# Weight blocks of twice the size in the merge of a hybrid encoder layer

## The chip, the cores and the metric

The kernel runs on one core of a Trainium2 chip. The metric is the device time of one execution in microseconds (us); the time before is the median of three runs. A further execution was recorded by the hardware profiler, and all rows come from it. The core's engines are TensorE (PE; its weight loads are shown as PEld), VectorE (DVE), ScalarE (ACT), GpSimd (POOL) and SyncE (SP, which here only issues transfers).

## The reference

One layer of a residual block on x of 2048 tokens by 1024 channels, float32:

```
h      = rms_norm(x, pre_mix_g)
proj   = h @ w_in                       # q, k, v | RWKV-7 inputs | two gates
y_a    = chunk_band_attention(q, k, v, rel_bias)
y_b    = rwkv7_time_mix(...)            # recurrent, a scan over time
merged = sigmoid(gA) * (y_a @ proj_a) + sigmoid(gB) * (y_b @ proj_b)
x      = x + rms_norm(merged @ w_out, post_mix_g)
hf     = rms_norm(x, pre_ffn_g)
x      = x + rms_norm(square(relu(hf @ w_up)) @ w_down, post_ffn_g)
```

proj_a and proj_b are 512 x 1024, and w_out is 1024 x 1024. The change concerns the lines `merged` and `merged @ w_out`.

## The kernel before

The tokens are worked in four groups of 512 (G). For each group come the recurrent part, the attention part and the merge; the feed-forward part follows once for each half of the tokens. Every product is made in three matmuls: an operand is kept as a rounded high part and a low part that holds the rest, and high x high, high x low and low x high are summed in PSUM (`mm3`, L74).

Weights come through `wsplit` (L58). It takes a raw buffer, loads the block on SP's queue (L63), and calls `split` (L69): ACT casts the block to the high part (whi, L70), DVE subtracts to get the low part (wlo, L71). Raw, high and low each have two buffers, shared by all weight blocks of this part of the program. A buffer is as large as its largest user, a block of `w_in` of 8 x 128 = 1,024 floats in each of 128 partitions.

The merge has two stages. In the first, `branch` (L1030) makes one block of 128 output channels of one branch: it loads the gate values (th, L1034, from gd), loads and splits a block of proj_b or proj_a of 4 x 128 = 512 floats a partition (L1035 and L1036), multiplies (12 matmuls of 512 columns into ps_p), and DVE applies the gate (L1039). `phase_attention` calls it eight times for the recurrent branch and stores the results (md, L1015) while the attention of the last heads still runs. `phase_merge` (L1042) calls it eight times for the attention branch, adds the stored result (mb, L1054 and L1056) and splits the sum into mh and ml (L1057). There are three buffers for th and three for mb.

In the second stage the output projection runs in two halves n of 512 columns, each over eight blocks k of w_out of 512 floats a partition (L1062), with 12 matmuls a block, three for each of four token tiles, into four PSUM banks (ps_o, L1066). At the end of a half ACT and DVE take the banks out (L1076, L1077).

Two other pieces of work are put between these blocks. `beside` is one set of operand sums for the feed-forward part (`combine`, L1110): its first step loads four tiles of 256 KB (cmb, L1145), its next three steps do one DVE subtraction each (L1117), and its fifth does the last one and stores four results on POOL's queue (L1141). `between` is `next_norm` (L295), the norm of the next group: its first step loads two tiles of x and the gains, 512 KB each (L302, L305), and each of the next four steps makes one tile (ACT L319, POOL, DVE L321, eight transposes on PE at L126, ACT L130 and DVE L131) and loads another tile of x while there is one. The last group has no next norm.

A scheduler orders the instructions of each engine by a simulated time, so that an instruction which is ready early may overtake others of its engine. Some are pinned: `keep_in_program_order` puts an instruction behind everything that was traced before it on its engine. The operand-sum loads, their DVE subtractions, the norm's loads and its first transposes are pinned so; weight, gate and mb loads are not. Each engine is given its instructions in the order that comes out of this.

Of the kernel before, what the change touches and what calls it, by code (L numbers as in the profile page):

```python
# [18 lines left out]
P = 128  # L19
D = 1024  # L20
KB = D // P
FF = 4096
HW = 512
NP = 4
# [18 lines left out]
def advance(steps, n=None):  # L43

    while n is None or n > 0:
        if next(steps, steps) is steps:
            return
        n = n and n - 1


class Block:
# [978 lines left out]
    def branch(self, y, br, i):  # L1030

        nc, mp = self.nc, self.bp
        t = mp.tile([P, G], F32, tag="th", bufs=3, name="th")
        nc.sync.dma_start(t, self.gd[br * KB + i])  # L1034
        w = self.a[("proj_a", "proj_b")[br]][:, i * P : (i + 1) * P]  # L1035
        wh, wl = self.wsplit(w.rearrange("(k p) n -> p k n", p=P), "w", NP, P)  # L1036
        ps = self.pd.tile([P, G], F32, tag="d", name="ps_p")
        self.mm3(ps, [(wh[:, k], wl[:, k], y[0][:, k], y[1][:, k]) for k in range(NP)])
        nc.vector.scalar_tensor_tensor(t, t, 1.0, ps, op0=ALU.add, op1=ALU.mult)  # L1039
        return t  # L1040

    def phase_merge(self, g, o, op, between, beside):  # L1042

        tc, nc, a = self.tc, self.nc, self.a
        with ExitStack() as ctx:
            e = ctx.enter_context
            cp = e(tc.tile_pool(name="mgc", bufs=1, reuse_waits="tile"))
            po = e(tc.tile_pool(name="mgpo", bufs=4, space=PSUM, reuse_waits="tile"))
            mh = cp.tile([P, KB, G], F32R, name="mh")
            ml = cp.tile([P, KB, G], F32R, name="ml")  # L1050
            gp = self.gain(op, a["post_mix_g"], "g_post")
            for i in range(KB):
                mb = self.bp.tile([P, G], F32, tag="mb", bufs=3, name="mb")
                nc.sync.dma_start(mb, self.md[i])  # L1054
                t = self.branch(self.ya, 0, i)
                nc.vector.tensor_tensor(t, t, mb, ALU.add)  # L1056
                self.split(mh[:, i], ml[:, i], t)  # L1057
            self.yctx.close()
            for n in range(2):
                ps = [po.tile([P, 512], F32, tag="o", name="ps_o") for _ in range(GT)]  # L1060
                for k in range(KB):
                    wh, wl = self.wsplit(a["w_out"][k * P : (k + 1) * P, None, n * 512 : (n + 1) * 512], "w", 1, 512)  # L1062
                    for t in range(GT):
                        ts = slice(t * P, (t + 1) * P)
                        for j, (l, r) in enumerate(((mh, wh), (mh, wl), (ml, wh))):
                            nc.tensor.matmul(  # L1066
                                ps[t], l[:, k, ts], r[:, 0], start=k == 0 and j == 0, stop=k == KB - 1 and j == 2
                            )
                    if n == 0 and k in (0, 3, 4, 5, 6):
                        advance(beside, 1)  # L1070
                    if n == 0 and k == 2 or n == 1 and k % 2 == 0:
                        advance(between, 1)
                ns = slice(n * 512, (n + 1) * 512)
                for t in range(GT):
                    sq = op.tile([P, 512], F32, tag="sqo", bufs=2, name="sqo")
                    nc.scalar.activation(sq, ps[t], AF.Square, accum_out=self.ssq[:, g, t, n : n + 1])  # L1076
                    nc.vector.tensor_tensor(o[t][:, ns], ps[t], gp[:, ns], ALU.mult)  # L1077
            advance(between)
# [426 lines left out]
```

## Time and profile before

| | us |
|---|---|
| median of three runs | 3324.03 (3318.0 to 3327.82) |
| the profiled execution's own time | 3325.37 |
| its span, first to last instruction | 3323.7 |
| PE busy | 3198.8 |
| DVE busy | 2248.2 |
| ACT busy | 1581.6 |
| POOL busy | 592.7 |
| output projection of the first group | 466.6 to 520.5 of the span |

In a row of groups, the source line, engine and operation come first, then what is written and read, the shape and the count; after the bar come busy time and mean duration in ns, and after the second bar the time that the engine idled just before these instructions, with what ended that idle time. In a timeline, a row has start, length, engine, line and tiles; "SPq" is an issue of a transfer by SP, not the transfer itself. Matmuls are pipelined and the profile models their ends, so PE's busy time is more than its work.

### The profile page before, as it was taken

The numbers are of one execution on the slowest core, as the hardware profiler recorded it, in microseconds if no ns is written. First come the engines' busy times: TensorE is split into PE (matmuls) and PEld (weight loads), VectorE is DVE, ScalarE is ACT, GpSimd is POOL, SyncE is SP. The second block draws the span as 40 slices with busy tenths as digits, with TensorE's granted clock in tenths as the row PEclk, the third lists the DMA queues.
The fourth block names the chain that finished last, engine by engine and source line by source line (L and its number), as shares of the span: only waits on it lengthen the run. The fifth ranks groups of instructions, "written<-read, shape, count | busy, mean of one in ns | idle before, by whom it ended". The sixth has DMA issues, their size and how long they took to land. (4 is left out here: it accounts for less than half of the span.)

```text
span 3323.7 us, 50325 instructions
## 1 busy us (share of the span) xinstructions
PE 3198.8 (96%) x18913; PEld 2597.9 (78%) x18913; DVE 2248.2 (68%) x3719; ACT 1581.6 (48%) x2575; POOL 592.7 (18%) x1093
## 2 busy tenths in 40 slices
PE   7999999999999999999999999999999999999998
PEld 5777778777877777877777787878788878788887
DVE  5775666786766876775876675777656757775565
ACT  3434634434644434654444663545543444454333
POOL 2222002222102222101222100121211112220000
PEclk9999999999999999999999999999999999999999
DMA  5335374247465336655325647664787875547565
GB/s 151 89 118 186 114 232 126 80 137 241 156 215 154 91 104 229 198 170 186 96 77 187 208 121 246 231 199 143 240 285 232 300 250 193 168 161 235 191 214 179
DMA packets 449692, 592.56 MB, mean 178 GB/s; under 512 B 26324, under 2 KB 313248, under 8 KB 449448
## 3 DMA queue, kind: packets, MB, share of 16 engines
q1 hardware_dynamic: 392488, 413.14, 40.1%
q0 software_dynamic: 47744, 159.42, 13.2%
q10 hardware_dynamic: 9216, 16.78, 1.4%
q8 instruction: 149, 2.44, 0.3%
q14 instruction: 95, 0.78, 0.1%
HBM read 425.37 MB, written 167.01 MB: 178 GB/s over the span
## 5 line engine op out<-in xcount | busy, mean ns | idle before, releaser
L1341 PE MATMUL ps_dn<-fop 128*128 128x512 f32 x2688 | 613.1, 390 | 2.3 <-DVE fop L71 1.5
L1341 PEld LDWEIGHTS ps_dn<-fop 128*128 128x128 f32 x2688 | 505.3, 188 | 108.2 <-DVE fop L71 2.2
L80 PE MATMUL psd<-hh,whi 128*128 128x512 f32 x1344 | 540.1, 402 | 10.8 <-ACT whi L70 7.6
L80 PE MATMUL psd<-hh,wlo 128*128 128x512 f32 x1344 | 538.1, 400 | 2.7 <-DVE wlo L71 2.6
L80 PE MATMUL psd<-hl,whi 128*128 128x512 f32 x1344 | 539.2, 401 | 0.0
L70 ACT CAST whi<-wraw 128x1024 fp32r<-128x1024 f32 (+1 forms) x296 | 255.5, 864 | 521.6 <-PE psd L80 337.2
L71 DVE TENSOR_TENSOR wlo<-wraw,whi 128x1024 fp32r<-128x1024 f32 (+1 forms) x296 | 292.8, 990 | 223.7 <-ACT whi L70 190.3
L80 PEld LDWEIGHTS psd<-hh,whi 128*128 128x128 f32 x1344 | 255.2, 190 | 61.7 <-ACT whi L70 8.4
L80 PEld LDWEIGHTS psd<-hh,wlo 128*128 128x128 f32 x1344 | 255.0, 190 | 55.1 <-DVE wlo L71 5.2
L80 PEld LDWEIGHTS psd<-hl,whi 128*128 128x128 f32 x1344 | 255.5, 190 | 48.9
L71 DVE TENSOR_TENSOR fop<-xraw,fop 128x1024 fp32r<-128x1024 f32 x112 | 137.1, 1224 | 175.0 <-ACT fop L70 174.3
L70 ACT CAST fop<-xraw 128x1024 fp32r<-128x1024 f32 x112 | 117.7, 1051 | 254.5 <-PE ps_dn L1341 187.5
L1223 POOL DMA_DIRECT2D xd<-X x192 | 103.7, 541 | 392.1 <-ACT X L1220 337.3
L71 DVE TENSOR_TENSOR fop<-wdraw,fop 128x1024 fp32r<-128x1024 f32 x112 | 136.7, 1221 | 23.5 <-ACT fop L70 22.7
L70 ACT CAST fop<-wdraw 128x1024 fp32r<-128x1024 f32 x112 | 117.7, 1051 | 39.8 <-DMA wdraw<-in_w_down_dram 26.1
L903 DVE CUSTOM_DVE_ANT_0 sc<-bias,ps_s 128x640 f32<-128x640 f32 (+4 forms) x128 | 94.0, 734 | 57.0 <-PE ps_pt L914 40.3
L919 DVE TENSOR_TENSOR PTl<-ps_pt,PTh 128x640 fp32r<-128x640 f32 (+4 forms) x128 | 94.4, 738 | 27.7 <-ACT PTh L918 27.2
L70 ACT CAST s12h<-s 128x1024 fp32r<-128x1024 f32 x32 | 33.7, 1052 | 163.7 <-PE ps_u L80 163.7
L908 ACT ACTIVATE sc<-sc,mn 128x640 f32<-128x640 f32 (+4 forms) x128 | 97.6, 762 | 26.1 <-DVE mn L903 25.7
L1066 PE MATMUL ps_o<-whi,mh 128*128 128x512 f32 x256 | 98.8, 400 | 10.2 <-ACT whi L70 8.5
L1066 PE MATMUL ps_o<-wlo,mh 128*128 128x512 f32 x256 | 101.8, 398 | 4.9 <-DVE wlo L71 4.8
L80 PE MATMUL ps_p<-yh,whi 128*128 128x512 f32 x256 | 101.3, 401 | 5.4 <-ACT whi L70 3.6
(368 smaller groups left out, 6823.5 us busy)
## 6 DMA issues: line engine op xcount, KB each, us to landing
wraw<-in_w_in_dram SPq DMA_DIRECT2D x168, 512.0 KB
xraw<-xd SPq DMA_DIRECT2D x112, 512.0 KB
xd<-X POOLq DMA_DIRECT2D x192, 256.0 KB, 5.3
wraw<-in_w_up_dram SPq DMA_DIRECT2D x80, 512.0 KB
wdraw<-wd SPq DMA_DIRECT2D x64, 512.0 KB
wdraw<-in_w_down_dram SPq DMA_DIRECT2D x48, 512.0 KB
gd<-gate ACTq DMA_DIRECT2D x64, 256.0 KB
wd<-cmb POOLq DMA_DIRECT2D x64, 256.0 KB, 3.5
```

The costliest lines, as they stand in the source:

```text
L70: high = self.nc.scalar.copy(hi, src)
L71: self.nc.vector.tensor_tensor(lo, src, hi.bitcast(F32), ALU.subtract)
L80: mm.append(nc.tensor.matmul(ps, l, r, start=n == 0, stop=n == last).ins)
L903: nc.vector.tensor_tensor_reduce(sc[:, 0:n], bias[:, s0:640], pss[:, c0 : c0 + n], 1.0, 3.0e38, ALU.add, ALU.min, mn,)
L908: nc.scalar.activation(sc[:, 0:n], sc[:, 0:n], AF.Exp, scale=-1.0, bias=mn, accum_out=sm[:, col : col + 1])
L919: nc.vector.tensor_tensor(lv, pst[:, 0:nk], hv.bitcast(F32), ALU.subtract)
L1066: nc.tensor.matmul(ps[t], l[:, k, ts], r[:, 0], start=k == 0 and j == 0, stop=k == KB - 1 and j == 2)
L1223: nc.gpsimd.dma_start(self.xd[q][i // 2][:, i % 2], src)
L1341: nc.tensor.matmul(ps, o[:, l, k, sl], o[:, r, k], start=start and n == 0, stop=stop and n == end)
```

## The change

Branch weights are loaded and split for two blocks i at a time, 4 x 256 floats a partition, and each of the two calls of `branch` uses its half. Blocks of the output projection are loaded and split for two k at a time, 2 x 512 floats. A block now fills its buffers. The numbers of matmuls and of floats loaded stay as they were. In the first half of the output projection the steps of the operand sums move from behind k = 0, 3, 4, 5, 6 to behind k = 2, 4, 5, 6, 7, and the first step of the next norm (its loads) moves from behind k = 2 to behind k = 4.

```diff
-        w = self.a[("proj_a", "proj_b")[br]][:, i * P : (i + 1) * P]
-        wh, wl = self.wsplit(w.rearrange("(k p) n -> p k n", p=P), "w", NP, P)
+        if i % 2 == 0:
+            w = self.a[("proj_a", "proj_b")[br]][:, i * P : (i + 2) * P]
+            self.bw = self.wsplit(w.rearrange("(k p) n -> p k n", p=P), "w", NP, 2 * P)
+        wh, wl = (x[:, :, i % 2 * P : (i % 2 + 1) * P] for x in self.bw)
...
                 for k in range(KB):
-                    wh, wl = self.wsplit(a["w_out"][k * P : (k + 1) * P, None, n * 512 : (n + 1) * 512], "w", 1, 512)
+                    if k % 2 == 0:
+                        w = a["w_out"][k * P : (k + 2) * P, n * 512 : (n + 1) * 512]
+                        wh, wl = self.wsplit(w.rearrange("(j p) n -> p j n", p=P), "w", 2, 512)
...
-                                ps[t], l[:, k, ts], r[:, 0], start=k == 0 and j == 0, stop=k == KB - 1 and j == 2
+                                ps[t], l[:, k, ts], r[:, k % 2], start=k == 0 and j == 0, stop=k == KB - 1 and j == 2
...
-                    if n == 0 and k in (0, 3, 4, 5, 6):
+                    if n == 0 and k in (2, 4, 5, 6, 7):
                         advance(beside, 1)
-                    if n == 0 and k == 2 or n == 1 and k % 2 == 0:
+                    if n == 0 and k == 4 or n == 1 and k % 2 == 0:
                         advance(between, 1)
```

## The prediction

> **What bounds the kernel now.** I read the page first, then the groups by line and form, the windows of the stages that the change touches, and the timelines of SP, ACT, DVE and PE inside one of them.
>
> ```profile
> span 3323.7 us, 50325 instructions
> PE 3198.8 (96%) x18913; PEld 2597.9 (78%) x18913; DVE 2248.2 (68%) x3719; ACT 1581.6 (48%) x2575; POOL 592.7 (18%) x1093
> L1066 PE MATMUL ps_o<-whi,mh 128*128 128x512 f32 x256 | 98.8, 400 | 10.2 <-ACT whi L70 8.5
> L80 PE MATMUL ps_p<-yh,whi 128*128 128x512 f32 x256 | 101.3, 401 | 5.4 <-ACT whi L70 3.6
> ```
>
> PE is busy in 96% of the span, so the number of matmuls sets the time, and an edit that removes no matmul can only win what PE idles. The change touches the branch products (ps_p) and the output projection (ps_o). There PE's idle time (the last column) ends with a cast (whi) or a subtraction (wlo) of a weight block. The answers on the two tiles give all of it for PE, in us and in number of stalls, and beside it stands how matmuls follow one another without a stall:
>
> ```profile
>   ACT whi L70: 8.5, 9
>   DVE wlo L71: 4.8, 7
> ...
>   ACT whi L70: 3.6, 5
> ...
>   DVE wlo L71: 0.3, 2
> ...
> 484.51 0.39 PE L1066 MATMUL ps_o<-whi,ml 128*128 128x512 f32 x1
> 484.74 0.39 PE L1066 MATMUL ps_o<-whi,mh 128*128 128x512 f32 x1
> 484.96 0.39 PE L1066 MATMUL ps_o<-wlo,mh 128*128 128x512 f32 x1
> 485.19 0.39 PE L1066 MATMUL ps_o<-whi,ml 128*128 128x512 f32 x1
> ```
>
> The first two rows are ps_o, the next two ps_p: 8.5 + 4.8 + 3.6 + 0.3 = 17.2 us. The other four rows show matmuls starting every (485.19 - 484.51) / 3 = 0.227 us while each is shown 0.39 long, so every stall really costs about 0.16 more than its idle time. The two stages look like this, four groups each (the branch stage first, then the output projection):
>
> ```profile
> 441.40:466.60 25.20, 23.38 (x96) 17.48 (x96) 18.74 (x29) 8.81 (x16) 0.54 (x1) 1.00 0.90 270
> 961.00:986.90 25.90, 25.04 (x105) 19.11 (x105) 19.03 (x31) 9.11 (x15) 1.08 (x2) 1.00 0.92 279
> 1475.00:1500.60 25.60, 25.23 (x107) 19.32 (x105) 19.43 (x31) 9.08 (x16) 1.08 (x2) 1.00 0.88 279
> 1997.00:2022.30 25.30, 24.03 (x104) 18.85 (x102) 18.38 (x30) 8.88 (x15) 0.85 (x2) 1.00 0.86 281
> 466.60:520.50 53.90, 50.26 (x226) 40.58 (x226) 29.65 (x42) 23.80 (x48) 5.62 (x14) 0.97 0.55 177
> 986.90:1037.80 50.90, 48.00 (x225) 39.12 (x225) 28.86 (x41) 23.34 (x47) 5.60 (x14) 1.00 0.56 180
> 1500.60:1553.50 52.90, 48.64 (x226) 39.14 (x225) 28.93 (x42) 23.19 (x48) 5.59 (x14) 1.00 0.55 178
> 2022.30:2072.80 50.50, 46.41 (x194) 35.60 (x193) 27.68 (x37) 21.92 (x38) 2.66 (x7) 1.00 0.72 226
> 497.66 1.04 PE L126 MATMUL pstr<-ident,xn 128*128 128x128 f32 x8
> ```
>
> Columns are length, then busy time with counts for PE, weight load, DVE, ACT and POOL, then granted clock, DMA share and GB/s. The output projection takes 53.9 + 50.9 + 52.9 + 50.5 = 208.2 us. Its floor is 4 x 192 matmuls x 0.227 = 174.3 plus 12 sets of eight transposes at 1.04 (last row; three groups with four sets) = 12.5. So at most about 21 us can be won there. The branch stage (25.2 to 25.9 against 96 x 0.227 = 21.8 and a few transposes) has DMA at 0.86 to 0.92: there the loads nearly fill the transfer engines.
>
> **The change part by part.**
>
> *First block of the output projection.* What SP issues, and what it does to the second block:
>
> ```profile
> 461.13 0.33 SPq L63 DMA_DIRECT2D wraw<-in_w_out_dram  x1
> 461.91 0.32 SPq L1034 DMA_DIRECT2D th<-gd  x1
> 462.28 1.84 SPq L1145 DMA_DIRECT2D cmb<-in_w_down_dram  x4
> 464.22 3.43 SPq L63 DMA_DIRECT2D wraw<-in_w_out_dram  x2
> 467.70 0.43 SPq L302 DMA_DIRECT2D x<-in_x_dram  x1
> 471.12 0.62 ACT L70 CAST whi<-wraw 128x512 fp32r<-128x512 f32 x1 [1.24 <-DMA wraw<-in_w_out_dram]
> 471.79 0.50 PE L1066 MATMUL ps_o<-whi,mh 128*128 128x512 f32 x1 [1.61 <-ACT whi L70]
> 991.15 0.50 PE L1066 MATMUL ps_o<-whi,mh 128*128 128x512 f32 x1 [1.51 <-ACT whi L70]
> 1505.52 0.49 PE L1066 MATMUL ps_o<-whi,mh 128*128 128x512 f32 x1 [1.98 <-ACT whi L70]
> 2026.62 0.51 PE L1066 MATMUL ps_o<-whi,mh 128*128 128x512 f32 x1 [1.05 <-ACT whi L70]
> ```
>
> Four operand-sum loads of 256 KB (462.28) stand between block k=0 and block k=1. The latter is issued at 464.22 and its cast starts at 471.12, 6.9 us later, and PE waits in every group: 1.61 + 1.51 + 1.98 + 1.05 = 6.15, with 4 x 0.16 = 6.8 us. After the change k=0 and k=1 are one load and k=2,3 goes ahead of the sums, so four blocks, 48 x 0.227 = 10.9 us of matmuls, are under way before a sum's load is in the queue. I take this whole term: **6.8 us**. What is behind the moved loads in SP's queue is the pair k=4,5, needed 10.9 us after the start; the moved megabyte takes 1.05 / 0.27 = 3.9 us at the branch stage's 270 GB/s. The norm loads (x, gain, x: three of 512 KB, 5.8 us at that rate) now stand ahead of pair k=6,7, needed 16.3 us in.
>
> *The remaining stalls of the output projection.* Idle left over: 8.5 - 6.15 + 4.8 = 7.15 in 9 + 7 - 4 = 12 stalls, with 12 x 0.16 that is 9.1 us. What makes them:
>
> ```profile
> 477.54 1.12 ACT L70 CAST whi<-wraw 128x512 fp32r<-128x512 f32 x2
> ...
> 478.58 1.28 DVE L321 SCALAR_TENSOR_TENSOR xn<-x,rs_r,g_pre 128x1024 f32<-128x1024 f32 x1 [1.29 <-POOL rs_r L107]
> 479.79 0.68 DVE L71 TENSOR_TENSOR wlo<-wraw,whi 128x512 fp32r<-128x512 f32 x1
> ...
> 480.53 0.67 PE L1066 MATMUL ps_o<-wlo,mh 128*128 128x512 f32 x1 [1.14 <-DVE wlo L71]
> 480.00:484.00 4.00, 3.47 (x9) 2.73 (x10) 2.28 (x4) 0.00 (x0) 1.15 (x2) 0.59 0.47 152
> L71 DVE TENSOR_TENSOR wlo<-wraw,whi 128x1024 fp32r<-128x1024 f32 x168 | 204.8, 1220 | 141.9 <-ACT whi L70 115.5 <-PE ps_yt L693 16.5 <-PE psd L80 9.8
> L70 ACT CAST whi<-wraw 128x1024 fp32r<-128x1024 f32 x168 | 176.2, 1049 | 363.9 <-PE psd L80 329.6 <-DVE X L557 15.5 <-DMA wraw<-in_w_in_dram 9.2
> L71 DVE TENSOR_TENSOR wlo<-wraw,whi 128x512 fp32r<-128x512 f32 x128 | 88.0, 688 | 81.8 <-ACT whi L70 74.8 <-PE psd L80 4.7 <-PE ps_rb L945 2.1
> L70 ACT CAST whi<-wraw 128x512 fp32r<-128x512 f32 x128 | 79.3, 620 | 157.7 <-PE ps_o L1066 57.8 <-DMA wraw<-in_proj_a_dram 40.2 <-DMA wraw<-in_w_out_dram 30.7
> ```
>
> The next group's norm (1.28 on DVE) sits in front of a block's subtraction, and PE, which has only the block in hand as cover, runs dry. A split may start when the block two before it is finished, so it has one block of PE time. Now that is 12 x 0.227 = 2.72 us for 0.620 + 0.688 = 1.31: slack 1.41, which one 1.28 and one 0.69 exceed. With pairs it is 5.44 us for 1.049 + 1.220 = 2.27: slack 3.17, room for the norm's 1.28 and two or three shorter ones. I take three quarters of 9.1, **6.8 us**, with bounds 0 and 9.1. The same stalls drop PE's clock: 0.59 of full in the 4 us from 480, a loss of 0.41 x 4 = **1.6 us**, which I count as won. [...]
>
> *The branches.* Idle 3.6 + 0.3 in seven stalls, 3.9 + 1.1 = 5.0 us. The two raw and two split buffers hold blocks of 512 elements in room for 1,024, so pairs let loads run twice as far ahead in time. But DMA is nearly full in this stage, and a pair needs 256 KB more on chip before its first matmul. I take half, **2.5 us**; bounds are 5.0 won and, below nothing, rival A.
>
> *Instructions saved.* 64 casts of 2 x 0.620 - 1.049 = 0.19 (12.2 us of ACT) and 64 subtractions of 2 x 0.688 - 1.220 = 0.16 (10.0 us of DVE), and 64 load issues of about 0.33 on SP. None of this is time of PE, which hides it; I cost it at 0. No row prices the longer runs of the branch weights (256 instead of 128 floats a row): from 270 / 0.90 = 300 GB/s at full share in the branch stage to 177 / 0.55 = 322 in the other, 7% of 2.1 MB a group, 0.5 us x 4 = 2 us at most; I take 0.
>
> *Moved steps.* The sums' DVE operations move one or two blocks later and still precede their stores on POOL, which nothing in this stage waits for. The norm's second tile was ready at 478.58 + 1.28 = 479.9 and the first transposes ran at 497.66, so 18 us cover a shift of two blocks (5.4 us). Were that cover gone, three groups would pay up to 1.28 each, 3.8 us.
>
> The sum is 6.8 + 6.8 + 1.6 + 2.5 = 17.7 us won. The profiled execution took 3325.37 us (span 3323.7), 1.3 above the median of 3324.03, so I subtract from the median: 3324.0 - 17.7 = **3306 us**.
>
> **The rivals.**
>
> *A, slower: the pair comes whole and late.* PE can't start a pair before 512 KB landed and a 1.049 cast ran: later by 262 KB / 270 GB/s = 0.97, plus 0.43, or 1.40 us for each of 16 pairs of the branch stage, 22.4 in all. Against it 6.8 stays won, so 3324 + 15.6 = 3340. It decides if SP issues a pair's load less than about 8 us ahead (6.9 as at 464.22, plus the longer cast), as when it is held behind a gate load (th) that waits for its buffer. Against it: at 461.13 the projection's block was issued before the last gate load at 461.91, so weights do overtake. Chance 0.09.
>
> *A2, slower: larger operations, longer bubbles.* If all 14 stalls on casts and 9 on subtractions stay, each grows by 0.43 or 0.53: 6.0 + 4.8 = 10.8, giving 3335. ACT's 23.8 and DVE's 29.65 of 53.9 us show neither full. [...] Against it the slack above, 3.17 instead of 1.41, which is for cover, not throughput. Chance 0.04.
>
> *B, no change to speak of: the stall moves to the first pair.* It lands at the end of the stage with DMA at 0.9, 1.40 later in each group, 5.6 of the 6.8 are lost, and of the later stalls half remain: 1.2 + 4.5, about 6 won, 3318. For it: the four branch windows have DMA at 0.86 to 0.92, so nothing lands early there. Against it: the moved megabyte no longer shares that stretch. Chance 0.20.
>
> *C, more:* all of 6.8 + 9.1 + 1.6 + 5.0 and the 2 for longer runs, 24.5, and a quarter of the 22.2 us of freed ACT and DVE time, 5, where that ends waits elsewhere: 3295. Chance 0.12.
>
> **How the numbers follow.** The forecast has 0.55. 0.3% of 3324, 10 us, is about what a measurement can tell from no change. The forecast and C lie beyond it: faster 0.55 + 0.12 = 0.67; B is the same, 0.20; A and A2 are slower, 0.13. The range runs from 3293 (C, a little beyond) to 3328 (B, the missing cover's 3.8 and four first branch pairs at 1.40), leaving out A, A2 and C's tail.
>
> **What would show it.** Right: no stall above 0.5 us before the first four blocks of the output projection in any group; its windows shorter by about 4 each; a 1.05 cast and a 1.22 subtraction, 64 each more; sums' loads behind the load of k=2,3; the clock 1.00 in the first group. Wrong: branch windows longer than 25.9, PE idle until a whi that ends with a proj load, or idle that comes back elsewhere in the span.

## The result and the profile after

The changed kernel took 3313.13 us (median of 8 runs, 3309.61 to 3317.83) against 3329.0 us for the kernel before (8 runs on the same chip, 3318.0 to 3341.9): ratio 0.9951, 95% interval 0.994 to 0.9962, about 16 us. The profiled execution took 3310.21 us. Its span is 15.2 us shorter than that of before. These are its page's span, PE's work and the projection's first product:

```profile
span 3308.5 us, 49983 instructions
PE 3188.2 (96%) x18913; PEld 2596.9 (78%) x18913; DVE 2242.7 (68%) x3655; ACT 1571.8 (48%) x2511; POOL 597.7 (18%) x1093
L1070 PE MATMUL ps_o<-whi,mh 128*128 128x512 f32 x256 | 101.8, 398 | 6.8 <-DVE o L1081 6.8
```

The matmuls are as many as before (18913), and 64 casts and 64 subtractions are gone. Where the row of before names whi as the end of PE's idle time, this one names o (L1081), the product that empties a bank at the end of a half. What ended PE's idle time before the output projection (us, number of stalls):

```profile
  DVE o L1081: 6.8, 1
  DVE wlo L71: 1.1, 2
```

and before the branch products:

```profile
  ACT yh L70: 2.7, 2
  DVE th L1041: 1.4, 3
  ACT whi L70: 0.9, 1
  DVE yl L71: 0.3, 1
```

Weight blocks now cost the projection 1.1 us of idle time in place of 8.5 + 4.8, and 6.8 us are a single new stall. It shows in the windows of the four projections (length, busy times with counts, then clock, DMA share, GB/s):

```profile
467.30:515.00 47.70, 47.60 (x226) 39.40 (x225) 29.40 (x36) 22.71 (x40) 6.54 (x15) 1.00 0.59 191
979.30:1027.20 47.90, 47.60 (x226) 39.45 (x226) 29.43 (x36) 22.75 (x40) 6.67 (x15) 1.00 0.57 194
1492.70:1541.10 48.40, 47.60 (x226) 39.40 (x226) 29.70 (x36) 22.71 (x40) 6.64 (x15) 1.00 0.59 192
2002.60:2056.00 53.40, 46.58 (x194) 37.74 (x194) 26.15 (x30) 19.82 (x30) 2.65 (x7) 0.94 0.65 203
```

The prediction shows the same four windows of the kernel before. Three fell from 53.9, 50.9 and 52.9 to 47.7, 47.9 and 48.4, 13.7 us together. The fourth, which has no next norm beside it, rose from 50.5 to 53.4. The four windows of the attention branch, cut for both kernels from its first matmul to the first of the projection, add up to this, before first, then after:

```profile
sum 96.50, PE 92.38 PEld 70.35 DVE 74.28 ACT 35.62 POOL 2.16; mean PE 23.09 PEld 17.59 DVE 18.57 ACT 8.90 POOL 0.54
```

```profile
sum 92.20, PE 90.32 PEld 71.05 DVE 69.35 ACT 29.53 POOL 2.71; mean PE 22.58 PEld 17.76 DVE 17.34 ACT 7.38 POOL 0.68
```

So 4.3 us came from there, and -13.7 + 2.9 - 4.3 = -15.1 us is nearly the whole difference of the spans. The recurrent, attention and feed-forward parts together add next to nothing to it.

**The new stall.** It can be followed through four engines in the last group. First PE, at the start of the second half of the projection, and POOL's stores of the operand sums:

```profile
2026.89 0.39 PE L1070 MATMUL ps_o<-wlo,mh 128*128 128x512 f32 x1
2034.10 0.79 PE L1070 MATMUL ps_o<-whi,mh 128*128 128x512 f32 x1 [6.82 <-DVE o L1081]
2034.69 0.63 PE L1070 MATMUL ps_o<-wlo,mh 128*128 128x512 f32 x1
```

```profile
2019.58 0.54 POOL L1145 DMA_DIRECT2D wd<-cmb  x1 [2.62 <-DVE cmb L1121]
2020.31 0.54 POOL L1145 DMA_DIRECT2D wd<-cmb  x1 [0.18 <-issue]
```

SP's loads of the feed-forward part's first operand (bl from ht, L1166; its high part bh is then cast from it by ACT) wait for these stores to land, in all, times and longest:

```profile
SPq L1166 <- DMA wd<-cmb: 7.5, 2, 6.3
```

Then ACT, and the taking out of the third and fourth bank by DVE:

```profile
2023.46 0.60 ACT L1080 ACTIVATE sqo<-ps_o 128x512 f32<-128x512 f32 x1
...
2031.14 1.04 ACT L1158 CAST bh<-bl 128x1024 fp32r<-128x1024 f32 x1 [6.99 <-DMA bl<-ht]
2032.09 0.59 ACT L1080 ACTIVATE sqo<-ps_o 128x512 f32<-128x512 f32 x1
...
2033.36 1.28 DVE L1081 TENSOR_TENSOR o<-ps_o,g_post 128x512 f32<-128x512 f32 x2
```

The scheduler put a cast of bl between the second and the third of the four ACT operations on the banks (sqo). Its load came late, so ACT stood 6.99 us in front of work that had long been ready. DVE took the third and the fourth bank out from 2033.36 on, and PE, which needs the third for the second half, went on at 2034.10. PE then runs at half rate, in steps of 0.43 us instead of 0.227 (granted clock 0.50 from 2035.60 to 2039.02). In the kernel before, the same casts stood behind all four sqo and a cast of whi:

```profile
2048.27 0.60 ACT L1076 ACTIVATE sqo<-ps_o 128x512 f32<-128x512 f32 x1
...
2049.99 0.61 ACT L1076 ACTIVATE sqo<-ps_o 128x512 f32<-128x512 f32 x1
...
2052.14 1.05 ACT L1154 CAST bh<-bl 128x1024 fp32r<-128x1024 f32 x1 [0.94 <-DMA bl<-ht]
```

There the loads of bl waited for the stores too, but less (SP's queue in this stage, before the change):

```profile
SPq L1162 <- DMA wd<-cmb: 1.5, 1, 1.5
```

### The profile page after: what moved, and what is told of

It is laid out like the page before. It is cut to its first block, busy times and chain, and to the rows that moved or that the text cites. A ratio compares the mean times of both kernels' runs of the same rounds, so it can differ in the third digit from the quotient of the medians.

```text
span 3308.5 us, 49983 instructions
## 1 busy us (share of the span) xinstructions
PE 3188.2 (96%) x18913; PEld 2596.9 (78%) x18913; DVE 2242.7 (68%) x3655; ACT 1571.8 (48%) x2511; POOL 597.7 (18%) x1093
## 5 line engine op out<-in xcount | busy, mean ns | idle before, releaser
L70 ACT CAST whi<-wraw 128x1024 fp32r<-128x1024 f32 x232 | 243.3, 1049 | 425.9 <-PE psd L80 330.4
L71 DVE TENSOR_TENSOR wlo<-wraw,whi 128x1024 fp32r<-128x1024 f32 x232 | 282.9, 1220 | 160.0 <-ACT whi L70 129.1
L918 ACT CAST PTh<-ps_pt 128x640 fp32r<-128x640 f32 (+4 forms) x128 | 79.9, 624 | 51.1 <-PE ps_pt L914 49.5
```

The source lines that it names most:

```text
L70: high = self.nc.scalar.copy(hi, src)
L71: self.nc.vector.tensor_tensor(lo, src, hi.bitcast(F32), ALU.subtract)
L918: nc.scalar.copy(hv, pst[:, 0:nk])
```

## The experiments

Batches of four ran on one chip each, beside runs of the kernel before: 3328.3 us (29 runs) in the first, 3327.2 (27) in the second, 3327.04 (11) in the third.

| run | median us (runs) | ratio, 95% interval |
|---|---|---|
| new places alone | 3328.35 (12) | 0.9991, 0.998 to 1.0002 |
| all pairs, old places | 3310.83 (5) | 0.9952, 0.994 to 0.9963 |
| branch pairs alone | 3318.1 (12) | 0.9974, 0.9965 to 0.9982 |
| projection pairs and new places | 3324.24 (12) | 0.9989, 0.9977 to 1.0001 |
| changed kernel again | 3315.05 (11) | 0.9969, 0.9956 to 0.9981 |
| bh casts behind the first half | 3311.24 (8) | 0.9958, 0.9942 to 0.9974 |
| sums at old places in the last group | 3313.86 (12) | 0.996, 0.9948 to 0.9973 |
| pairs, split in halves | 3308.69 (9) | 0.9953, 0.9939 to 0.9968 |
| halves, bh casts later | 3304.62 (6) | 0.993, 0.9916 to 0.9944 |
| pairs, bh casts later | 3306.46 (6) | 0.9937, 0.9922 to 0.9953 |

**The new places alone** (blocks as before):

```diff
-                    if n == 0 and k in (0, 3, 4, 5, 6):
+                    if n == 0 and k in (2, 4, 5, 6, 7):
...
-                    if n == 0 and k == 2 or n == 1 and k % 2 == 0:
+                    if n == 0 and k == 4 or n == 1 and k % 2 == 0:
```

> Blocks of 512 floats as before; only the operand-sum steps (now behind k = 2, 4, 5, 6, 7) and the next norm's loads (behind k = 4) are moved. My theory: of the 17.7 us, the wait for block k = 1 (6.8 us over four groups) belongs to the place of the sums' loads, the rest to the larger blocks; so about 6 us less than before, ratio 0.998, PE's idle time until whi on ps_o down from 8.5 to about 2.5 us, until wlo still near 4.8. Rival: the order alone does it all, ratio 0.995. Rival: with small blocks the later sums crowd the same slack, ratio 1.000.

The ends of PE's idle time before the projection in this run:

```profile
  DVE wlo L71: 5.7, 10
  ACT whi L70: 3.3, 5
  DVE o L1077: 2.5, 3
```

The wait for casts falls from 8.5 to 3.3 us, near the 2.5 expected, but subtractions (4.8 to 5.7) and the taking out of the banks (o, 1.7 to 2.5) take some of it back: 11.5 us in place of 15.0. In the time, this can't be told from nothing.

**All pairs, old places:**

```diff
-                    if n == 0 and k in (2, 4, 5, 6, 7):
+                    if n == 0 and k in (0, 3, 4, 5, 6):
...
-                    if n == 0 and k == 4 or n == 1 and k % 2 == 0:
+                    if n == 0 and k == 2 or n == 1 and k % 2 == 0:
```

> Pairs of blocks in the branches and in the output projection; sums' steps and norm loads at the places of before (behind k = 0, 3, 4, 5, 6 and k = 2). My theory: the sums' megabyte now stands between pair k = 0,1 and pair k = 2,3, which is needed 5.4 us later where block k = 1 was needed 2.7 us later and came 1.2 to 2.2 us late; so the early waits go too or shrink to under 1 us a group, and about 10 to 14 us are won, ratio 0.996 to 0.997. Rival (the order is what counts): the wait moves to k = 2 with its old size, about 7 us won, ratio 0.998.

It has the gain of the whole change, a little more than the theory expected. Before the projection's matmuls PE idles 1.6 us in three stalls, all for wlo. In the last group it waits here too, 3.47 us for bh and 0.47 for bl from 2031 on: the first feed-forward matmuls stand between the two halves, and on ACT a cast of bl stands between the first and the second sqo.

**Branch pairs alone** (the projection as before):

```diff
-                    if k % 2 == 0:
-                        w = a["w_out"][k * P : (k + 2) * P, n * 512 : (n + 1) * 512]
-                        wh, wl = self.wsplit(w.rearrange("(j p) n -> p j n", p=P), "w", 2, 512)
+                    wh, wl = self.wsplit(a["w_out"][k * P : (k + 1) * P, None, n * 512 : (n + 1) * 512], "w", 1, 512)
```

> Only the branch weights in pairs; the output projection and the places as before. My theory after the two traces: PE's idle time until a branch weight falls from 3.9 to about 1 us, but gate values take its place (1.4 us until th in the trace after), so 0 to 3 us won, ratio 0.999 to 1.000. Forecast of the prediction: 2.5 us. Rival A of the prediction: 22 us lost, ratio 1.006.

```profile
  DVE wlo L71: 8.3, 8
  DVE o L1079: 1.9, 1
  ACT whi L70: 1.2, 2
```

These rows are again PE's idle time before the projection, whose code is the old one. The wait for casts is nearly gone (8.5 to 1.2): with the branch weights in pairs the first load of w_out goes out at 454.38, 12.5 us before PE needs it (466.9), where before it was 461.13 and 466.6. The sums' loads still stand between the first two blocks, but all of them are early now. The stalls on subtractions stay and grow (4.8 to 8.3); a split still has one block of cover. The gain is 0.9974, about 8.7 us, where 0 to 3 was expected: the four windows of the attention branch add up to 92.8 us in place of 96.5, and the four of the projection, whose code is unchanged, to 204.3 in place of 208.2.

**Projection pairs and new places, branches as before:**

```diff
-        if i % 2 == 0:
-            w = self.a[("proj_a", "proj_b")[br]][:, i * P : (i + 2) * P]
-            self.bw = self.wsplit(w.rearrange("(k p) n -> p k n", p=P), "w", NP, 2 * P)
-        wh, wl = (x[:, :, i % 2 * P : (i % 2 + 1) * P] for x in self.bw)
+        w = self.a[("proj_a", "proj_b")[br]][:, i * P : (i + 1) * P]
+        wh, wl = self.wsplit(w.rearrange("(k p) n -> p k n", p=P), "w", NP, P)
```

> Only the output projection in pairs, with the new places; branch weights in blocks of 512. My theory: nearly all of the gain is here, 12 to 16 us, ratio 0.995 to 0.996, with PE's idle time until whi on ps_o near 0. Rival (a pair of w_out needs the branch pairs' room ahead of it): a first stall at each start of the output projection of 1 to 2 us, ratio 0.998.

```profile
  ACT whi L70: 5.2, 4
  DVE o L1079: 4.3, 1
  DVE wlo L71: 1.1, 4
```

The expected 12 to 16 us don't show in the time; what shows is the rival named with it. Four stalls on casts, one at the start of each projection: this is also the prediction's rival B. The load of k=0 and 1 is issued at 460.64, 6.5 us before PE's first matmul (467.15), and in the changed kernel at 453.88, 13.4 us before. The projection's own four windows are short all the same, 195.6 us in place of 208.2, but the windows of the attention branch ahead of them, which end with these stalls, grew from 96.5 to 102.7, and this execution lost its clock more (0.987). So the projection's pairs need those of the branches, which let SP run further ahead. The row on o is here too: the stall of the last group came with these pairs, though the branch blocks are the old ones.

**The changed kernel again**, for the spread and the place of the stall:

> The changed kernel itself, for comparison on the same chip and for a second profile. Ratio to before 0.995 as at first. My theory of the clock: half-rate stretches of 3.4 or 6.8 us come from windows in which PE idles much, and where they fall varies from one execution to the next, so the profile again shows some 20 to 27 us lost to them, in part at other places. Rival: the changed kernel loses its clock at the same places each time. The 7 us stall in the last group's output projection should be there again, since it lies in the order of ACT's queue.

The stall is there again (6.1 us for o, at 2043.6). The span is 3318.8 us, 10.3 longer than in the other profile of the same kernel, and what differs is the clock, 0.992 in the first and 0.989 here: 0.008 x 3308.5 = 26.5 us lost to it in the first and 0.011 x 3318.8 = 36.5 in the second, 10.0 of the 10.3. Of the seven half-rate stretches of the first execution between 100 and 3300 us six came at the same places again, one did not, and seven came elsewhere.

**The bh casts behind the evacuation of the first half** (the last of its four sqo):

```diff
-                    nc.scalar.activation(sq, ps[t], AF.Square, accum_out=self.ssq[:, g, t, n : n + 1])
+                    self.evac[n] = nc.scalar.activation(sq, ps[t], AF.Square, accum_out=self.ssq[:, g, t, n : n + 1]).ins
...
-            advance(self.first_half(0, bp))
+            with tc.issue_after(self.evac[0]): advance(self.first_half(0, bp))
```

> The changed kernel, with the feed-forward part's first casts (bh) queued on ACT behind the taking out of the first half of the output projection. My theory: the 7 us stall in the last group goes, and the half-rate stretch right behind it, 7 to 9 us less than the changed kernel, ratio to before 0.992 to 0.993. Rival: the casts only move and PE waits for bh at the start of the feed-forward part or for another evacuation, ratio 0.995.

The stall on o is gone. One of 2.85 us on whi and one of 0.65 on wlo come instead, in the last group: the late bh casts now stand in front of the casts of w_out's next blocks. The casts had moved by a few places, not far enough, and the time is the rival's.

**The sums at their old places in the last group:**

```diff
-                    if n == 0 and k in (2, 4, 5, 6, 7):
+                    if n == 0 and k in ((2, 4, 5, 6, 7) if g + 1 < self.NG else (0, 3, 4, 5, 6)):
```

> The changed kernel, with the operand-sum steps at the old places (behind k = 0, 3, 4, 5, 6) in the last group alone. My theory: the stall of 7 us comes from the sums' stores, which land later and hold the bl loads on SP's queue; with early sums the loads go out some 5 us earlier and the stall shrinks to 2 us or less, ratio to before 0.993 to 0.994. Rival (the sums have nothing to do with it): stall as before, ratio 0.995.

The projection's own idle falls to 0.7 us, but PE waits 3.41 us for bh, until 2037.55, and 0.77 for bl: the scheduler has put the first feed-forward matmuls between the two halves. The stall is shorter, but the last window is still 51.3 us, and the time is no better. So the later sums make the stall longer, but they are not why there is one; the kernel with all pairs and old places has it too, with a window of 51.7.

**Pairs loaded whole, cast and subtracted in two instructions of 512 each:**

```diff
-        self.split(hi, lo, raw)
+        for h in (halves or [(slice(None), slice(None), slice(None))]): self.split(hi[h], lo[h], raw[h])
...
+            self.bw = self.wsplit(w.rearrange("(k p) n -> p k n", p=P), "w", NP, 2 * P, halves=[(slice(None), slice(None), slice(j * P, j * P + P)) for j in (0, 1)])
...
+                        wh, wl = self.wsplit(w.rearrange("(j p) n -> p j n", p=P), "w", 2, 512, halves=[(slice(None), j, slice(None)) for j in (0, 1)])
```

> Pairs are loaded as in the changed kernel, but cast and subtracted in two instructions of 512 floats each, so buffers and loads run as far ahead as with pairs while ACT and DVE get the 128 instructions of before. Theory of cover (mine): the gain stays, ratio 0.994 to 0.996, PE's stalls on ps_o stay near those of the changed kernel. Rival (fewer, larger instructions make the gain): 22 us of ACT and DVE time come back and stalls with them, ratio 0.998 or more. [...]

PE has no idle time at all before the projection's matmuls. The last group's stall has moved between the halves:

```profile
2022.25 0.39 PE L1070 MATMUL ps_o<-whi,ml 128*128 128x512 f32 x1
2027.97 0.79 PE L80 MATMUL ps_u<-bh,a1h 128*128 128x512 f32 x1 [5.34 <-ACT bh L1158]
2029.23 0.79 PE L80 MATMUL ps_u<-bl,a1h 128*128 128x512 f32 x1 [0.47 <-DVE bl L1159]
```

So saving 64 casts and 64 subtractions is not what won the time. With all of them back the kernel is no slower than the changed one beside it (0.9953 against 0.9969, intervals overlapping). What is left is that two blocks are loaded and split while PE has two blocks to work on. No run keeps blocks of 512 floats and gives them more buffers, so the look-ahead isn't told apart from the larger loads. The smaller instructions leave fewer stalls: the two profiles with halves have none on wlo before the projection's matmuls, the six with all pairs whole 0.7 to 3.2 us. Whether that makes the kernel faster, the time is too close to show.

**Halves, with the bh casts later.** In the last group ACT's casts of bl are queued behind the cast for blocks k=4 and 5 of the second half:

```diff
-        for h in (halves or [(slice(None), slice(None), slice(None))]): self.split(hi[h], lo[h], raw[h])
+        for h in (halves or [(slice(None), slice(None), slice(None))]): self.cast = self.split(hi[h], lo[h], raw[h])
...
-                        advance(between, 1)
+                        self.behind = self.cast if k < 6 else self.behind; advance(between, 1)
...
-            advance(self.first_half(0, bp))
+            with tc.issue_after(self.behind): advance(self.first_half(0, bp))
```

> Pairs with casts and subtractions in halves of 512, and in addition the casts of the last group's feed-forward operands (bh) are queued on ACT behind the cast of blocks k=4 and 5 of the second half of the output projection. Theory (these casts stand too early in the queues, in front of the evacuation or in front of PE's next blocks): the wait of 5.5 + 1.03 us of PE on ps_u<-bh at 2028 is gone, the last group's output projection falls from 53.1 to about 48 us, nothing else moves, and the ratio to the kernel before is about 0.993 (3303 to 3306 us). Rival (the feed-forward part needs bh right after the projection and its casts now come late): PE waits 2 to 6 us on bh at the start of the feed-forward part instead, and the ratio stays at 0.995. Half-rate stretches of the clock can move either by several us, so the windows and the stalls decide, not the time alone.

```profile
472.00:519.10 47.10, 47.10 (x225) 39.35 (x224) 28.72 (x41) 22.98 (x46) 6.15 (x14) 1.00 0.56 190
984.00:1031.20 47.20, 47.20 (x225) 39.35 (x225) 29.06 (x42) 23.19 (x46) 6.07 (x14) 1.00 0.57 193
1496.50:1543.70 47.20, 47.20 (x226) 39.41 (x225) 28.89 (x41) 23.08 (x46) 6.39 (x14) 1.00 0.56 186
2006.10:2049.60 43.50, 43.50 (x193) 36.03 (x192) 25.69 (x35) 20.15 (x36) 2.55 (x6) 1.00 0.77 246
```

PE is busy for the whole of all four windows. The last takes 43.5 us, and 192 x 0.227 is 43.6: with this number of matmuls there is nothing left to win in this stage. Nothing came back at the start of the feed-forward part; the longest idle time there, up to 2100, is 0.91 us. Its median is the lowest of all, and the theory's 3303 to 3306 us holds.

**Pairs, with the bh casts later** (the same edit on the changed kernel):

> The changed kernel with the same shift of the bh casts on ACT, and casts and subtractions of whole pairs. Theory: the wait of 6.8 us for the product o in the last group's output projection goes, its window falls from 53.3 to about 48 us, ratio 0.993 to 0.995. Rival (the larger operations get in each other's way): one or two waits of 2 to 3 us on whi or wlo of the last pair take its place, as in the run with the casts behind the evacuation, and the ratio stays near 0.996; then the run with halves should show less of it.

```profile
2037.52 0.60 ACT L1080 ACTIVATE sqo<-ps_o 128x512 f32<-128x512 f32 x1 [2.34 <-PE ps_o L1070]
...
2039.62 0.60 ACT L1080 ACTIVATE sqo<-ps_o 128x512 f32<-128x512 f32 x1
...
2046.77 1.05 ACT L70 CAST whi<-wraw 128x1024 fp32r<-128x1024 f32 x1 [5.47 <-DMA wraw<-in_w_out_dram]
2047.72 3.89 ACT L1158 CAST bh<-bl 128x1024 fp32r<-128x1024 f32 x4
```

All four sqo now come together, the four bh casts where ACT has time, and the projection's idle is 1.1 us in two stalls. The last window falls to 43.5 us, and the ratio is the one expected. Whole pairs and halves differ by 1.8 us in the median, with overlapping intervals. The cause of the new stall is shown: the place of a few casts in ACT's queue. Why the scheduler chose that place is not.

**The projection pairs a second time**, for the low clock of its first profile (0.987 over 3325.4 us):

> The kernel with pairs in the output projection alone, profiled a second time. If its large clock loss (mean clock 0.987 over 3325 us, about 43 us) belongs to the kernel, half-rate stretches come at the same places and the clock is 0.986 to 0.988 again; if it was that execution's, the clock is 0.990 or more and the span shorter by about 33 us for each 0.01 of clock, so about 3315 at 0.990.

The clock was 0.991 and the span 3319.9, not the expected 3315: the low clock was that execution's. But the clock alone gives back about 13 us and the span fell by 5.5 only. The branch windows were longer this time (27.06 and 28.41 us in the first two groups against 25.30 and 26.65); why stays open. In both profiles they are longer than the 25.0 and 24.1 of the kernel before.

**The kernel before a second time:**

> The kernel before, profiled a second time. Theory: the places of half-rate stretches change from execution to execution, and the idle of PE before weight blocks does not (whi 8.5 and wlo 4.8 us on ps_o, within 2 us); the span differs from 3323.7 by about 33 us for each 0.01 of mean clock. Rival (a stall of 1 to 2 us of PE sets them off): the stretches at 252, 480.7, 736.7, 1675, 1771, 1887 and 2402 come at the same places again.

The stalls on weight blocks are those of the first profile: 8.4 us in nine on whi, 5.3 in nine on wlo. Of seven half-rate stretches between 100 and 3300 us five came at the same places again (251, 736, 1678, 1773, 1886), two did not (480.7 and 2402), and two came elsewhere (1254.6, 2828). So neither is quite right: the places recur, the stretches need not. The first group's projection, at half rate from 480.7 in the first profile, kept its full clock in this one.

## Why the prediction was right, and where it was not

The forecast was 17.7 us, the ratio gives about 16 and the profiled spans 15.2. By its steps:

- *The wait for the second block (6.8).* Gone in all four groups: no stall over 0.3 us before the first four blocks. The order of loads is as predicted; SP's issues in the first group are k=0 and 1, k=2 and 3, the sums, k=4 and 5:

```profile
453.88 0.38 SPq L63 DMA_DIRECT2D wraw<-in_w_out_dram  x1
...
458.92 0.38 SPq L63 DMA_DIRECT2D wraw<-in_w_out_dram  x1
...
464.21 1.80 SPq L1149 DMA_DIRECT2D cmb<-in_w_down_dram  x4
466.12 0.38 SPq L63 DMA_DIRECT2D wraw<-in_w_out_dram  x1
```

  The step gave this to the moved loads. They are enough, since alone they take the 8.5 to 3.3, with none of it at the second block, but they are not needed: the pairs do it with the sums in either place, and the branch pairs alone take the 8.5 to 1.2. With 13.4 us of lead for the first pair rivals A and B did not come.
- *The remaining stalls (6.8 of 9.1).* Undersized. The three undisturbed windows fell by 13.7 us, of which 0.41 x 4 = 1.6 is clock, so 12.1 us in three groups; with the stall repaired the fourth falls by 7.0. That is 19.1 in all against 6.8 + 6.8. The step left out the row of 1.7 us on o in two stalls, at the end of a half, which is gone too once the new stall is repaired; and it held back a quarter for the norm, though 0 to 1.1 us on weight blocks is all that is left in the two repaired kernels. With the row on o the stalls make 8.5 + 4.8 + 1.7 + 18 x 0.16 = 17.9; where the other 1.2 come from is not shown.
- *The clock (1.6).* 1.00 in the first group, as predicted, and 1.00 in all of the first three projections in the changed kernel and in the two repaired ones, where the kernel before has 0.97 in the first. It is not a gain of the whole kernel: the mean clock is 0.993 before and 0.992 after, a second execution of before had no half rate there, and the last group lost its clock.
- *The branches (2.5).* Undersized: 4.3 in the windows of the attention branch, near the upper bound of 5.0, and alone they are worth about 8.7 us in the time, since they also bring the projection's first blocks early. The projection's pairs, which the forecast gave most of the sum, were worth little without them (0.9989, with an interval up to 1.0001).
- *Instructions saved (0).* Right: with all of them put back the time is no worse.
- *Moved steps (0).* **This step failed.** Its reason was that nothing in this stage waits for the stores of the sums. In the last group SP's loads of the feed-forward operands do, and did before (1.5 us). A cast that waits for these loads stood ahead of the third sqo, and PE lost 6.82 us and then half its rate for five more. The last group's window is 53.4 - 43.5 = 9.9 us longer than it has to be. The moved steps are only part of this: at the old places the window is still 51.3 or 51.7. In every kernel with pairs in the projection whose bh casts were left alone, PE waits 3.4 to 6.8 us there; with the old blocks, at either place, it waits at most 1.9. So what the sum put at nothing without a reason is the order of ACT's queue in the last group. The prediction followed the norm past the moved steps, and not the feed-forward part's first casts, which stand inside this stage before and after.

So the total was right in part by luck, because errors nearly cancel: the stalls and the branches were worth more than forecast, and a stall of 9.9 us with its clock was not foreseen: 13.7 + 7.0 + 4.3 - 9.9 = 15.1. One of the prediction's signs of being wrong, idle time that comes back, did show. The two kernels in which that stall is repaired show it in the time: they gain 20.6 and 22.4 us in the median, where the changed kernel gains 15.9 and, the second time, 12.2.

## What to carry to other kernels

Blocks that left half of their buffers empty let loads run less far ahead here: the first load for the projection went out 5.5 us before PE's first matmul there (461.13 and 466.6), and in the changed kernel 13.4 us before (453.88 and 467.3). So fill the buffers before counting instructions saved, and do it for the stage before as well, since its blocks decide when the first load goes out (with the branch pairs alone at 454.38). After an edit that makes a stage shorter, look at where the scheduler now puts operations on late data: one of them at the head of an engine's queue held up everything behind it here (ACT, 6.99 us), and it is found by reading that queue's rows around the stall. Compare executions by the stalls and windows, not by spans alone, while the clock takes 20 to 43 us in each, as in these 14 (mean clock 0.994 to 0.987).

## What the runs showed of the hardware

In the first executions of before and of the changed kernel the clock falls to half in stretches of 3.41 or 6.83 us, seven in each between 100 and 3300 us. These windows of the first execution of before are the stretch at 480.7 and the 3.41 us ahead of it:

```profile
477.29:480.70 3.41, 1.63 (x7) 0.85 (x6) 2.12 (x4) 1.37 (x4) 0.75 (x2) 1.00 0.00 1
480.70:484.12 3.42, 3.42 (x9) 2.68 (x10) 1.58 (x3) 0.00 (x0) 1.15 (x2) 0.50 0.60 193
```

In its second execution the same wait for wlo (1.14 us) fell otherwise:

```profile
476.28:479.69 3.41, 3.41 (x16) 2.47 (x14) 1.73 (x2) 2.28 (x4) 1.27 (x3) 1.00 0.26 94
479.69:483.11 3.42, 2.28 (x10) 1.61 (x9) 3.25 (x5) 0.00 (x0) 0.61 (x1) 1.00 0.25 71
483.11:486.52 3.41, 3.41 (x16) 2.81 (x15) 1.29 (x2) 0.96 (x2) 1.03 (x2) 1.00 0.79 260
```

In the 3.41 us ahead of the stretch PE is busy for 1.63 us in seven matmuls, and then runs at a clock of 0.50. In the window that holds the wait in the second execution it is busy for 2.28 us in ten, and the clock stays at 1.00. The difference is not the wait for wlo but a second one: in the first execution PE had also waited 0.65 us for whi, until 478.19, and in the second it did not. So waits of 0.65 and 1.14 us stood ahead of this stretch; that they made it is my reading, and how much idle time it takes was not shown, since no run changes one wait alone.

Between the two profiles of the changed kernel the clock made 10.0 of the 10.3 us.
